# Residual products and the first tiles behind them by token halves, with half norms between

## The chip, the cores and the metric

The kernel runs on one core of a Trainium2 chip. The metric is the device time of one launch in microseconds (us). The core has five engines that run their own instruction queues: TensorE (PE, matrix products; its weight loads are listed as PEld), VectorE (DVE), ScalarE (ACT), GpSimd (POOL) and SyncE (SP, which here issues all DMAs).

## What is computed

One step of a diffusion backbone: two layers over 640 tokens (128 of context, 512 latent), width 1024. Each layer is

```
h = h + gate_a * Mixer(RMSNorm(h) * (1 + scale_a) + shift_a)
h = h + gate_f * SwiGLU(RMSNorm(h) * (1 + scale_f) + shift_f)
```

and a final RMSNorm gives the output. Scale, shift and gate have one value per channel for the context tokens and one for the latent ones. The mixer projects the normed input to many column tiles (`misc`, `mq`, `ckv`, ...), runs three branches (latent attention, gated linear attention, gated DeltaNet) and ends in an output projection (`wo`). The feed-forward part multiplies by 2 x 2816 columns (`fg`, `fu`) and back by `fo`. All of it is in float32.

## The kernel before

Activations lie transposed: channels on the 128 partitions, 640 tokens along the free dimension. The residual `h` is eight tiles of 128x640. A token half is 320 columns, `HS[0]` and `HS[1]`; half 0 holds the 128 context tokens and 192 latent ones, so an operation with a per-channel factor needs two pieces there (128 and 192 columns) and one (320) in half 1 (`PIECES`).

A float32 product is made of three float32r products: the weight tile is split into a rounded part `wh` (ACT, L465) and the residue `wl` (POOL, L466), the activations into `xh` and `xl`, and `mm_k` (L469) issues xh*wh, xl*wh, xh*wl for each token half and each 128 rows of depth.

`Stream` (L284) holds all large products as a list of units in a fixed order. A unit is up to four depth steps of one output tile, for one token half (c is 0 or 1) or for both (c is None), and it uses one block of weights of 128x512. `step` emits one depth step, `to(name)` emits until that tile is done and its post-operation is emitted, `steps(n)` emits n steps. Blocks are loaded by DMA into three buffers `wr` (on the SP queue) and split into three buffer pairs `wh`, `wl`; `ahead` (L319) splits one block ahead. Products write to a ring of three PSUM tiles of two banks. A unit with halves "in" or "post" runs half 0 and then half 1 with the same weight blocks.

The order in which each engine takes its instructions is fixed before the run by the framework's planner, from the order of emission and from its own idea of when each instruction is ready. While the chip runs, each engine's queue is strictly in order.

A residual product is followed by a norm that the next product needs. There are four such joins: `wo` to `fg0` in each layer, `fo1` of layer 0 to `misc` of layer 1, and `fo1` of layer 1 to the final norm and the output. Before the change a join goes like this (`resid_posts` L640, `join` L655):

- tiles 0 to 6 of the residual product run whole; after each, `h_update` (L637, DVE, reads PSUM) adds it to `h`, `Norm.add` squares it (L597, ACT) and adds the square to `nacc` (L598, DVE). `prescale` (L613, ACT) multiplies the tile by the next scale; at the `fo1` joins this is done in place, and in layer 0 only after `h` has been written to DRAM (`hsp`).
- tile 7 runs by halves. After each half: `h_update` of the half, its square (L602, ACT), two products with a matrix of ones that sum over channels (`cs`, L607, PE), then 1/sqrt by a logarithm and an exponential (L486, L488, ACT, each with a load of its function table).
- `modulate` (L615) makes the next input, for each of eight tiles and each half: the product with 1/rms (L619 on DVE, for tiles 1, 3, 5 on POOL; L622 on DVE for tile 7), the shift and rounding to `xh` (L624, ACT), the residue `xl` (L631, DVE). At the last join the product with 1/rms (L1810) is the output and goes out by DMA.
- the first tile behind the join (`fg0` or `misc`) runs by halves with shared weight blocks, all others whole.

In layer 0 `ModVe` (L549, DVE) also computes modulation values beside `wo0` to `wo4`, and `mod_fix` (L564, L567) finishes them before `prescale` can start.

Of the kernel before, what the change touches and what calls it, by code (L numbers as in the profile page):

```python
# [30 lines left out]
GROUPS = ((0, 11), (11, 22))  # L31

# [247 lines left out]
def mark(s):  # L280
    pass


class Stream:  # L284
    """Matrix products in a fixed order, emitted piece by piece between other work."""

    def __init__(self, pieces, load, split, psum, mm, ring):
# [3 lines left out]
        for name, ap, k0, kn, xs, c, first, last, post in pieces:  # L291
            if (name, k0) not in seen:
                seen[name, k0] = len(self.subs)
                self.subs.append((ap, kn))
                self.uses.append(0)
            i = seen[name, k0]
            self.uses[i] += 1
            self.units.append((name, i, k0, kn, xs, c, last, post))
# [20 lines left out]
    def ahead(self):  # L319
        i, c = self.units[self.u][1], self.units[self.u][5]  # L320
        self._split(i)
        top = max(self.w)
        for j in range(1, 3):
            self._load(top + j)
        if len(self.w) < self.ring and (top == i or c == 1):
            self._split(top + 1)

    def step(self):
# [8 lines left out]
        if self.k == kn:  # L337
# [5 lines left out]
            if last and (ph or c in (None, 1)):  # L343
                ps = self.ps[name] if c == 0 else self.ps.pop(name)
                ps = ps[:, :, :HF]
                with self.prio("pp"):
                    if ph:
                        self.posts[name](ps, c)
                    else:
                        self.posts.pop(name)(ps)  # L350
                if c != 0:
                    self.done.add(name)
                else:
                    self.done.add(name + "/0")
        return 0.82 if c is None else 0.41

    def steps(self, n):
        for _ in range(n):
            self.step()
# [13 lines left out]
def tile_hybrid(ctx: ExitStack, tc, a):  # L373
# [127 lines left out]
    # ---- modulation  # L501
# [20 lines left out]
    class ModVe:  # L522
        """Products of the condition with rows of the modulation weights, in single steps of the vector engine."""
# [59 lines left out]
    # ---- residual, norms  # L583
# [3 lines left out]
    class Norm:  # L587
        def __init__(self):
            self.acc = sp.tile([P, T], F32, name="nacc", tag="nacc", bufs=1)
            self.ps = self.last = None  # L590
# [8 lines left out]

        def end(self, h, c):  # L600
# [3 lines left out]
        def fin(self, c):  # L604
            self.ps = psg("cs") if self.ps is None else self.ps
            for i, t in enumerate((self.acc, self.last)):
                pe.matmul(self.ps[:, c, :HF], ones, t[:, HS[c]], start=(i == 0), stop=(i == 1))  # L607
            rstd_from(self.ps[:, c, :HF], self.acc[:, HS[c]], 1.0 / D, epsD[:, 0:1])

    def prescale(us, hs, sc, ds=range(7)):  # L610
        for d in ds:
            for i, s, e in ((0, 0, TP), (1, TP, T)):
# [27 lines left out]
    def resid_posts(names, hs, g, nm, keep=False):  # L640
        def post(ps, c=None, d=0):
            if d < 7:
                h_update(hs, d, ps, g)
                nm.add(d, hs[d])
                if keep:
                    dma(hsp[d], hs[d])
            else:
                h_update(hs, d, ps, g, (c,))
                nm.end(hs[d], c)
                if keep:  # L650
                    dma(hsp[d][:, HS[c]], hs[d][:, HS[c]])
        for d in range(8):
            G.posts[names[d]] = lambda ps, c=None, d=d: post(ps, c, d)

    def join(name, hs, nm, after, pre=None):  # L655
        """The last residual tile, the norm and its use, by halves of the tokens."""
        if pre:
            pre()
        G.to(name + "/0")
        G.steps(5)  # L660
        nm.fin(0)
        G.to(name)
        after(0, range(4))
        nm.fin(1)
        after(0, range(4, 8))
        after(1, range(8))

    # ---- DRAM scratch
# [8 lines left out]
    # ---- gated DeltaNet  # L677
# [142 lines left out]
    def turn_pairs(src, dst, scale):  # L820
        """Both heads of a pair from channels to tokens, chunk by chunk."""
# [13 lines left out]
    def gdn_solve(lp):  # L835
        Bb = lp.tile([P, 10, P], F32, name="Bb")
        ge.memset(Bb, 0.0)
        for d in range(2):
# [26 lines left out]
            for f in range(2):  # L865
# [11 lines left out]
                def narrow(w):  # L877
                    """Bb[:, g].T @ w[:, g] for all g, by the narrow operand and a turn."""
# [150 lines left out]
    # ---- latent attention  # L1029
# [225 lines left out]
    # ---- gated linear attention  # L1255
# [184 lines left out]
    # ---- the order of the large products  # L1440
    pieces = []

    def job(name, src, kt, xs, halves=None, ks=None):
        ks = ks or [(k0, min(4, kt - k0)) for k0 in range(0, kt, 4)]
        for c in ((0, 1) if halves else (None,)):
            for k0, kn in ks:
                pieces.append((name, src[:, k0 * P:(k0 + kn) * P], k0, kn, xs, c, k0 == 0, k0 + kn == kt, halves == "post"))

    for l in range(L):
        def k8(n, halves=None, ks=None, l=l):  # L1450
# [9 lines left out]
        else:  # L1460
            k8("misc", "in")
            k8("mq0")
# [24 lines left out]
        for d in range(8):  # L1487
            k8(f"wo{d}", "post" if d == 7 else None)
        for gi, (f0, f1) in enumerate(GROUPS):
            for f in range(f0, f1):  # L1490
                k8(f"fg{f}", "in" if f == 0 else None)
                k8(f"fu{f}")
            for d in range(8):
                job(f"fo{gi}_{d}.{l}", a["wfo"][l, d, :, f0 * P:f1 * P], f1 - f0, ("a",),
                    "post" if (gi, d) == (1, 7) else None)
# [42 lines left out]
    # ---- the layers  # L1538
# [36 lines left out]
    for l in range(L):  # L1575
# [166 lines left out]
        resid_posts([f"wo{d}.{l}" for d in range(8)], hs, mod[:, 16:24], nm)  # L1742
        for d in range(7):
            G.to(f"wo{d}.{l}")
            if l == 0:
                mv.run(0, range(16 + OPT["mc"] + (24 - OPT["mc"]) * min(d, 5) // 5, 16 + OPT["mc"] + (24 - OPT["mc"]) * min(d + 1, 5) // 5))
        if l == 0:
            mod_fix(mod, prm, 3)
            mod_fix(mod, prm, 4)
        mark(f"normf{l}")  # L1750
# [93 lines left out]
```

## Time and profile before

| what | value |
|---|---|
| median of 3 runs | 2895.22 us (2894.1 to 2898.76) |
| span of the profiled execution | 2896.0 us; no other time is listed for it |
| busy PE / PEld / DVE / ACT / POOL | 94% / 86% / 53% / 42% / 41% |
| mean granted TensorE clock | 0.968 |
| DMA | 317.10 MB, mean 109 GB/s |

Busy times are shares of the span. Products on PE overlap, so a busy PE is not a PE at its full rate: how many it does is read from when the tiles end. The granted clock is 1.00 at 2.4 GHz and 0.50 at 1.2 GHz.

### The profile page before, as it was taken

What the parts mean: (1) busy time and instruction counts of PE and PEld (TensorE: products, weight loads), DVE (VectorE), ACT (ScalarE), POOL (GpSimd) and SP (SyncE); (2) the same over time, 40 slices, a digit from 0 to 9 for tenths busy, and PEclk for the clock granted to TensorE, in tenths of its full rate; (3) what the DMA queues carried; (4) which work ended last, traced back from release to release, by engine and by line L of the source; (5) the groups of instructions that cost most, each with busy time, mean ns of one, the idle gap of its engine ahead of it and who ended that gap; (6) DMA issues with size and microseconds to landing.
All of it is one profiled execution on the core that took longest, in us unless ns stands there. A gap on an engine that the chain in (4) does not pass through costs nothing. (4 is left out here: it accounts for less than half of the span.)

```text
span 2896.0 us, 49763 instructions
## 1 busy us (share of the span) xinstructions
PE 2721.4 (94%) x19444; PEld 2498.5 (86%) x19444; DVE 1542.6 (53%) x2834; ACT 1209.0 (42%) x2276; POOL 1196.0 (41%) x872
## 2 busy tenths in 40 slices
PE   7899999889999999999998899987999999999998
PEld 4788888778779899999988888876877898999998
DVE  4765584747655699177358576556334334211212
ACT  5575655543333522122366645554333344222223
POOL 3543222333325467366445323233333264443443
PEclk9999999999999999999999999998999999999999
DMA  6254433245433355344323534332423231222222
GB/s 207 90 161 141 91 82 94 88 130 168 140 101 127 108 189 177 86 139 156 105 84 110 177 90 97 72 93 73 137 79 88 73 111 59 77 73 78 73 74 83
DMA packets 291834, 317.10 MB, mean 109 GB/s; under 512 B 163696, under 2 KB 174768, under 8 KB 291472
## 3 DMA queue, kind: packets, MB, share of 16 engines
q1 hardware_dynamic: 291600, 313.92, 37.3%
q8 instruction: 154, 2.52, 0.4%
q14 instruction: 80, 0.66, 0.1%
HBM read 266.01 MB, written 47.82 MB: 108 GB/s over the span
## 5 line engine op out<-in xcount | busy, mean ns | idle before, releaser
L466 POOL TENSOR_TENSOR wl<-wr,wh 128x512 fp32r<-128x512 f32 (+1 forms) x576 | 813.9, 1416 | 1307.0 <-ACT wh L465 1177.0
L474 PE MATMUL gm<-xh,wh 128*128 128x320 f32 x3456 | 846.2, 322 | 25.1 <-ACT xh L624 9.4
L474 PE MATMUL gm<-xh,wl 128*128 128x320 f32 x3456 | 826.8, 316 | 13.4 <-POOL wl L466 13.4
L474 PE MATMUL gm<-xl,wh 128*128 128x320 f32 x3456 | 832.5, 317 | 7.2 <-DVE xl L631 4.2
L465 ACT ACTIVATE wh<-wr 128x512 fp32r<-128x512 f32 (+1 forms) x576 | 357.6, 623 | 944.0 <-PE gm L474 648.9
L474 PEld LDWEIGHTS gm<-xh,wh 128*128 128x128 f32 x3456 | 589.6, 192 | 52.5 <-ACT xh L624 14.5
L474 PEld LDWEIGHTS gm<-xl,wh 128*128 128x128 f32 x3456 | 594.3, 192 | 25.0 <-DVE xl L631 9.8
L474 PEld LDWEIGHTS gm<-xh,wl 128*128 128x128 f32 x3456 | 592.6, 192 | 21.7 <-POOL wl L466 15.5
L549 DVE CUSTOM_DVE_ANT_0 ctb<-wmt,cbb 128x1024 f32<-128x1024 f32 (+1 forms) x200 | 298.6, 1493 | 3.4
L637 DVE SCALAR_TENSOR_TENSOR h<-gm,mod,h 128x128 f32<-128x128 f32 x144 | 55.7, 462 | 272.2 <-PE gm L474 266.1
L474 PE MATMUL gm<-ah,wh 128*128 128x320 f32 x704 | 164.6, 310 | 0.5 <-DVE h L637 0.5
L474 PE MATMUL gm<-ah,wl 128*128 128x320 f32 x704 | 164.1, 309 | 0.0
L474 PE MATMUL gm<-al,wh 128*128 128x320 f32 x704 | 163.9, 309 | 0.0
L962 ACT ACTIVATE VN<-ch 64x64 f32<-64x64 f32 x320 | 70.0, 219 | 178.5 <-DVE vs L959 164.5
L474 PEld LDWEIGHTS gm<-ah,wh 128*128 128x128 f32 x704 | 118.7, 188 | 1.6 <-DVE h L637 1.5
L474 PEld LDWEIGHTS gm<-al,wh 128*128 128x128 f32 x704 | 118.5, 188 | 0.2
L474 PEld LDWEIGHTS gm<-ah,wl 128*128 128x128 f32 x704 | 118.5, 188 | 0.0
L1773 DVE TENSOR_TENSOR th<-th,gm 128x640 f32<-128x640 f32 x44 | 36.2, 822 | 149.2 <-PE gm L474 148.4
L1766 DVE SCALAR_TENSOR_TENSOR th<-th,gm 128x640 f32<-128x640 f32 x44 | 35.9, 816 | 138.3 <-ACT th L1765 138.3
L479 POOL TENSOR_TENSOR al<-th,ah 128x640 fp32r<-128x640 f32 x44 | 89.5, 2033 | 28.0 <-DVE ah L478 28.0
L474 PE MATMUL gm<-ol,wh 128*128 128x320 f32 x384 | 99.3, 332 | 1.5 <-POOL ol L479 1.5
L474 PE MATMUL gm<-oh,wh 128*128 128x320 f32 x384 | 98.7, 334 | 0.5 <-DVE gth L1524 0.3
(747 smaller groups left out, 3822.8 us busy)
## 6 DMA issues: line engine op xcount, KB each, us to landing
wr<-in_wall_dram SPq DMA_DIRECT2D x432, 256.0 KB, 3.0
wmt<-in_wmodt_dram SPq DMA_DIRECT2D x60, 512.0 KB, 3.7
wr<-in_wfo_dram SPq DMA_DIRECT2D x64, 256.0 KB, 2.6
wr<-in_wbr_dram SPq DMA_DIRECT2D x48, 256.0 KB, 2.7
wmt<-in_wmodt_dram SPq DMA_DIRECT2D x40, 256.0 KB, 3.2
wm<-in_wmod_dram SPq DMA_DIRECT2D x16, 512.0 KB, 8.3
wr<-in_wfo_dram SPq DMA_DIRECT2D x32, 192.0 KB, 2.4
h<-in_xt_dram SPq DMA_DIRECT2D x16, 320.0 KB, 5.5
```

The lines of the kernel that those rows point to most:

```text
L465: se.activation(wh[:, :w], wr[:, :w], AF.Copy)
L466: ge.tensor_tensor(wl[:, :w], wr[:, :w], wh[:, :w], op=ALU.subtract)
L474: pe.matmul(ps[:, c, :HF], w_[:, wsl], x_[kx][:, c * HF:(c + 1) * HF], start=(start and i == 0), stop=(stop and i == 2))
L479: (lo or ge).tensor_tensor(dst_l, src, dst_h, op=ALU.subtract)
L549: ins = ve.tensor_tensor_reduce(self.t, wm, self.c[:, i], 0.5, 0.0, ALU.mult, ALU.add, accum_out=acc[h][:, m - m0, i:i + 1])
L637: ve.scalar_tensor_tensor(hs[d][:, s:e], ps[:, c, s - c * HF:e - c * HF], g[:, d, i:i + 1], hs[d][:, s:e], op0=ALU.mult, op1=ALU.add)
L962: se.activation(VN[d * 64:(d + 1) * 64, h, n], ps[h * 64:(h + 1) * 64, 1], AF.Copy)
L1766: ve.scalar_tensor_tensor(v3(th), v3(th), 1.0, ps, op0=ALU.add, op1=ALU.mult)
L1773: ve.tensor_tensor(v3(th), v3(th), ps, op=ALU.mult)
```

## The change

The last three tiles of each residual product (`NHV = 3`) run by halves: half 0 of tiles 5, 6, 7, then half 1 of tiles 5, 6, 7. Each half has its own PSUM tile, its own post-operation and its own copy of the weight blocks (the key of a block now holds the half). Likewise the first two tiles behind a join run as half 0 of both, then half 1 of both, again with their own copies of the blocks: `fg0` and `fu0`, and `misc` and `mq0` in layer 1. After each half of tiles 5 and 6 its square is added to `nacc` by half (`Norm.part`) and the half is prescaled. `join` now emits half 0's norm one depth step into half 1 of tile 5, all eight tiles of half 0's `modulate` between the next steps, and half 1's norm and `modulate` after half 1 of tile 7. `ahead` splits two blocks ahead for units by halves. The sums of the norm go to the small PSUM pool.

```diff
     def ahead(self):
...
-        if len(self.w) < self.ring and (top == i or c == 1):
-            self._split(top + 1)
+        want = i + (1 if c is None else 2)
+        while len(self.w) < self.ring and max(self.w) < want and max(self.w) + 1 < len(self.subs):
+            self._split(max(self.w) + 1)
...
+        def part(self, h, c):
+            sq = tmp()
+            se.activation(sq[:, HS[c]], h[:, HS[c]], AF.Square)
+            ve.tensor_tensor(self.acc[:, HS[c]], self.acc[:, HS[c]], sq[:, HS[c]], op=ALU.add)
...
-    def join(name, hs, nm, after, pre=None):
-        if pre:
-            pre()
-        G.to(name + "/0")
-        G.steps(5)
+    def join(name, l, nm, after):
+        G.to(f"{name}7.{l}:0")
+        G.steps(1)
         nm.fin(0)
-        G.to(name)
-        after(0, range(4))
+        for i in range(4):
+            after(0, range(2 * i, 2 * i + 2))
+            G.steps(2)
+        G.to(f"{name}7.{l}:1")
+        G.steps(1)
         nm.fin(1)
-        after(0, range(4, 8))
         after(1, range(8))
...
+    def by_halves(jobs, own):
+        for c in range(2):
+            for name, src, kt, xs in jobs:
+                for k0 in range(0, kt, 4):
+                    kn = min(4, kt - k0)
+                    key = f"{name}:{c}"
+                    pieces.append((key if own else name, src[:, k0 * P:(k0 + kn) * P], k0, kn, xs, c, k0 + kn == kt, own, key))
...
-        for d in range(8):
-            k8(f"wo{d}", "post" if d == 7 else None)
+        for d in range(8 - NHV):
+            k8(f"wo{d}")
+        by_halves([w8(f"wo{d}") for d in range(8 - NHV, 8)], True)
         for gi, (f0, f1) in enumerate(GROUPS):
...
+            if gi == 0:
+                by_halves([w8("fg0"), w8("fu0")], False)
```

## Rows read from the trace of the kernel before

**Rows 1.** The page: busy time of PE, and the granted clock in 40 slices.
```profile
PE 2721.4 (94%) x19444; PEld 2498.5 (86%) x19444; DVE 1542.6 (53%) x2834; ACT 1209.0 (42%) x2276; POOL 1196.0 (41%) x872
PEclk9999999999999999999999999998999999999999
```

**Rows 2.** Windows at layer 1's `wo` join: length, busy time by engine, clock, DMA.
```profile
2380.00:2403.00 23.00, 22.65 (x150) 21.72 (x148) 6.65 (x15) 11.32 (x19) 7.79 (x6) 1.00 0.23 66
2403.00:2432.00 29.00, 23.57 (x104) 19.45 (x105) 18.36 (x38) 18.43 (x37) 11.31 (x10) 0.76 0.15 43
```

**Rows 3.** Timeline of DVE there: start, duration, instruction, idle time before it.
```profile
2380.21 1.14 DVE L637 SCALAR_TENSOR_TENSOR h<-gm,mod,h 128x128 f32<-128x128 f32 x3 [4.28 <-PE gm L474]
2387.25 1.14 DVE L637 SCALAR_TENSOR_TENSOR h<-gm,mod,h 128x128 f32<-128x128 f32 x3 [4.28 <-PE gm L474]
...
2397.82 0.68 DVE L637 SCALAR_TENSOR_TENSOR h<-gm,mod,h 128x128 f32<-128x128 f32 x2 [0.76 <-PE gm L474]
...
2405.32 0.49 DVE L619 TENSOR_TENSOR th<-us,nacc 128x320 f32<-128x320 f32 x1 [1.85 <-ACT nacc L488]
...
2424.40 1.68 DVE L631 SCALAR_TENSOR_TENSOR xl<-th,mod,xh 128x320 fp32r<-128x320 f32 x2 [1.18 <-ACT xh L624]
...
2431.70 0.82 DVE L1773 TENSOR_TENSOR th<-th,gm 128x640 f32<-128x640 f32 x1 [2.91 <-PE gm L474]
```

**Rows 4.** Timeline of ACT there: the square of a half.
```profile
2398.53 0.47 ACT L602 ACTIVATE th<-h 128x320 f32<-128x320 f32 x1 [1.71 <-DVE h L637]
```

**Rows 5.** Windows of the modulate stage, layer 1's `wo` join and `misc` join.
```profile
2405.00:2426.10 21.10, 16.86 (x62) 13.26 (x63) 16.77 (x35) 14.11 (x31) 7.49 (x7) 0.68 0.04 12
1456.00:1477.30 21.30, 17.09 (x63) 13.84 (x63) 18.98 (x36) 15.08 (x33) 8.82 (x9) 0.68 0.12 36
```

**Rows 6.** The same windows, weight residues (L466) on POOL alone.
```profile
2405.00:2426.10 21.10, 1.28 (x1) 0.68 0.04 12
1456.00:1477.30 21.30, 3.08 (x3) 0.68 0.12 36
```

**Rows 7.** Tile `wr`, 2375 to 2405 us: splits (ns) and DMA landing.
```profile
L465 ACT ACTIVATE wh<-wr x8: 620/632/632, 2376.4 to 2402.9; 128x512 fp32r<-128x512 f32 x8
L466 POOL TENSOR_TENSOR wl<-wr,wh x8: 1261/1296/1306, 2377.2 to 2403.6; 128x512 fp32r<-128x512 f32 x8
DMA to landing us min/median/max: 2.5/2.6/3.0
```

**Rows 8.** Timeline of DVE at layer 0's `wo` join.
```profile
952.02 1.14 DVE L637 SCALAR_TENSOR_TENSOR h<-gm,mod,h 128x128 f32<-128x128 f32 x3 [0.66 <-PE gm L474]
...
1002.62 0.82 DVE L1773 TENSOR_TENSOR th<-th,gm 128x640 f32<-128x640 f32 x1 [2.91 <-PE gm L474]
```

**Rows 9.** Timeline of ACT at that join: the first prescale.
```profile
958.62 1.31 ACT L613 ACTIVATE us<-h,mod 128x128 f32<-128x128 f32 x3 [2.69 <-DVE mod L567]
```

**Rows 10.** Timeline of DVE at the `misc` join (layer 0's `fo1`).
```profile
1425.03 1.14 DVE L637 SCALAR_TENSOR_TENSOR h<-gm,mod,h 128x128 f32<-128x128 f32 x3 [6.91 <-PE gm L474]
...
1449.23 0.68 DVE L637 SCALAR_TENSOR_TENSOR h<-gm,mod,h 128x128 f32<-128x128 f32 x2 [2.08 <-PE gm L474]
1456.78 1.20 DVE L619 TENSOR_TENSOR th<-h,nacc 128x320 f32<-128x320 f32 x1 [0.59 <-ACT nacc L488]
1475.54 1.70 DVE L631 SCALAR_TENSOR_TENSOR xl<-th,mod,xh 128x320 fp32r<-128x320 f32 x2 [1.15 <-ACT xh L624]
```

**Rows 11.** Timeline of ACT there: prescale, then the copies of `misc` and `mq0`.
```profile
1450.06 1.02 ACT L613 ACTIVATE h<-h,mod 128x128 f32<-128x128 f32 x2 [3.76 <-DMA hsp<-h]
1478.40 0.69 ACT L1598 ACTIVATE misc<-gm 128x640 f32<-128x640 f32 x1
1485.52 0.69 ACT L1618 ACTIVATE th<-gm 128x640 f32<-128x640 f32 x1
```

**Rows 12.** Timeline of PE and DVE near the end.
```profile
2878.16 0.41 PE L474 MATMUL gm<-ah,wh 128*128 128x320 f32 x1 [0.23 <-DVE h L637]
2883.96 0.55 DVE L637 SCALAR_TENSOR_TENSOR h<-gm,mod,h 128x320 f32<-128x320 f32 x1
```

More of the change, by code (lines that the diff above doesn't have):

```diff
@@ L31 @@
 GROUPS = ((0, 11), (11, 22))
+NHV = 3
 O_MQ, O_CKV, O_KR = 0, 256, 384
@@ L290, in __init__ @@
         seen = {}
-        for name, ap, k0, kn, xs, c, first, last, post in pieces:
-            if (name, k0) not in seen:
-                seen[name, k0] = len(self.subs)
+        for name, ap, k0, kn, xs, c, last, post, key in pieces:
+            if (key, k0) not in seen:
+                seen[key, k0] = len(self.subs)
                 self.subs.append((ap, kn))
                 self.uses.append(0)
-            i = seen[name, k0]
+            i = seen[key, k0]
             self.uses[i] += 1
@@ L358, in steps @@
         for _ in range(n):
-            self.step()
+            if self.u < len(self.units):
+                self.step()
     def fill(self, us):
@@ L1460, in tile_hybrid @@
         else:
-            k8("misc", "in")
-            k8("mq0")
+            by_halves([w8("misc"), w8("mq0")], False)
             k8("mq1")
@@ L1741, in tile_hybrid @@
         nm = Norm()
[L1742 to L1750, printed above, removed]
         with pool("us", "left") as up:
             us = [up.tile([P, T], F32, name=f"us{d}") for d in range(7)]
-            join(f"wo7.{l}", hs, nm, lambda c, ds: modulate(hs, nm.acc, mod[:, 32:40], mod[:, 24:32], c, ds, us),
-                 lambda: prescale(us, hs, mod[:, 32:40]))
+            resid_posts("wo", l, hs, mod[:, 16:24], nm,
+                        halved=lambda d, c: prescale(us, hs, mod[:, 32:40], range(d, min(d + 1, 7)), c))
+            for d in range(8 - NHV):
+                G.to(f"wo{d}.{l}")
+                if l == 0:
+                    mv.run(0, range(16 + OPT["mc"] + (24 - OPT["mc"]) * min(d, 5) // 5, 16 + OPT["mc"] + (24 - OPT["mc"]) * min(d + 1, 5) // 5))
+            if l == 0:
+                mod_fix(mod, prm, 3)
+                mod_fix(mod, prm, 4)
+            mark(f"normf{l}")
+            prescale(us, hs, mod[:, 32:40], range(8 - NHV))
+            join("wo", l, nm, lambda c, ds: modulate(hs, nm.acc, mod[:, 32:40], mod[:, 24:32], c, ds, us))
         with pool("fp", "left") as fp:
@@ L1797, in tile_hybrid @@
                 m2 = mods[l + 1]
-                join(f"fo1_7.{l}", hs, nm, lambda c, ds: modulate(hs, nm.acc, m2[:, 8:16], m2[:, 0:8], c, ds, hs[:7]),
-                     lambda: prescale(hs, hs, m2[:, 8:16]))
+                G.to(f"fo1_{7 - NHV}.{l}")
+                prescale(hs, hs, sc_n, range(8 - NHV))
+                join("fo1_", l, nm, lambda c, ds: modulate(hs, nm.acc, m2[:, 8:16], m2[:, 0:8], c, ds, hs[:7]))
             else:
@@ L1811, in result @@
                         dma(a["yt"][d][:, HS[c]], t[:, HS[c]])
-                def scaled():
-                    for d in range(7):
-                        se.activation(hs[d], hs[d], AF.Copy, scale=fn[:, d:d + 1])
-                join(f"fo1_7.{l}", hs, nm, result, scaled)
+                G.to(f"fo1_{7 - NHV}.{l}")
+                prescale(hs, hs, sc_n, range(8 - NHV))
+                join("fo1_", l, nm, result)
         mvctx.__exit__(None, None, None)
```

80 lines of the change are left out of this document (44 added, 36 removed).

## The prediction

> **What bounds the kernel now.** I read the page first. PE is busy for 94% of the span, and its clock stands at 9 in nearly every slice [rows 1]; the other engines are near half or below. So time can only be won where PE does not run at its full rate, and the four joins are such places. The windows show it next: in the 23 us ahead of layer 1's `wo` join PE handles 150 products at a clock of 1.00, in the 29 us behind it 104 at 0.76, while DVE rises from 6.65 to 18.36 us and ACT from 11.32 to 18.43 [rows 2]. Then the timeline of DVE gives the steps of a join, because `h_update` starts as soon as a tile is done. Two whole `wo` tiles end 7.04 us apart [rows 3]: 48 products, 0.1467 us each. This is the full rate.
>
> From the end of `wo4` (2380.21) to the end of `fu0` (2431.70) pass 51.5 us [rows 3]. The 240 products in it need 240 x 0.1467 = 35.2 us; 16.3 us are lost. The same rows divide the time:
>
> - A, tiles 5, 6 and half 0 of tile 7: 2380.21 to 2397.82, 17.6 us, PE at full rate.
> - B, half 0's chain (update, square, sums, logarithm, exponential): to 2405.32, 7.5 us. PE does half 1 of tile 7 under it.
> - C, `modulate` of both halves: to 2424.40 + 1.68 = 2426.08, 20.8 us. DVE is busy for 16.8 of 21.1 us, ACT for 14.1, PE's clock is 0.68 [rows 5]. DVE and its exchange with ACT set the pace; PE waits for each `xh` and `xl`.
> - D, what PE still has to do: to 2431.70, 5.6 us.
>
> Layer 0's `wo` join takes 50.6 us between the same points [rows 8]. The `misc` join, from the end of `fo1_4` (1425.03), takes 53.4 us to the end of `misc` and 60.5 us to that of `mq0` [rows 10, 11].
>
> **The change part by part.** I go by layer 1's `wo` join and then say what differs at the others.
>
> A shrinks: half 0's chain starts after 72 products, 72 x 0.1467 = 10.6 us instead of 17.6. That is the gain, 7.0 us; the products taken out are not saved, they now lie under B and C, where PE had idle time.
>
> B keeps its instructions. Under it ACT gets a half square of tile 5 (0.47, as in [rows 4]), a half prescale of about the same size, and weight splits: a block now serves 12 products, 1.76 us, instead of 3.52, so some 2 splits more of 0.63 [rows 7]. That is 2.2 us more on ACT, in order, in a chain that also waits for DVE and PE. Between 0 and 2.2 I take 1.0, since the chain leaves gaps: B = 8.5. The sums of half 0 are now emitted one depth step into half 1 of tile 5. Behind a late square, PE has the rest of half 1 queued; but PE then has 10.6 us of products for 8.5 us of chain plus the first of C, so this wait costs nothing unless it passes 2 us.
>
> C keeps all of `modulate` and gains two things on DVE. First, the updates of half 1 of tiles 6 and 7 (0.55 each [rows 12]) and one half addition (0.49, as a 128x320 product in [rows 3]): 1.6 us. Second, the weights. The join has 10 blocks more than before: 6 for `wo5` to `wo7`, 4 for `fg0` and `fu0`. When C begins, 8.5 us after half 0 of tile 7, PE has used 8.5 / 1.76 = 4.8 blocks of half 1 and two are split ahead, so 7 of the 14 blocks that follow half 0 are still to be split, against one in the window of before [rows 6]. What a residue on POOL does to DVE the trace shows by comparison: the stage at the `misc` join has 3 residues instead of 1 and the same `modulate`, and DVE is busy for 18.98 us instead of 16.77 [rows 5, 6]. That is 1.1 us of DVE for each residue; the stage was no longer for it (20.8 us there too, less 0.3), because DVE had idle time. With 6 more residues, 6.6 us, that idle time is used up: 16.8 + 1.6 + 6.6 = 25.0 us with DVE never idle. Below this stands 20.8 (all of it falls into idle time), above it 20.8 + 1.6 + 6.6 = 29.0 (the idle time stays). I take 25.0, the nearest to what the two stages show. Half 1's chain starts when PE ends half 1 of tile 7, 10.6 + 1 us after half 0, and needs 8.5: it is done about 20 us after half 0. C's half 0, with two pieces a tile, is more than half of 25.0 and lasts until 8.5 + 12.5 = 21 at least. So it is hidden, but only if its sums are not queued on PE behind a depth step of `fg0` that waits for a late `xl`.
>
> D shrinks. The last `xl` releases one depth step of `fg0` and then half 1 of `fu0`: 27 x 0.1467 = 4.0 us, instead of 5.6.
>
> The supply of weights: a `wr` buffer comes round after DMA 2.6, ACT 0.63 and POOL 1.30 us, with 0.2 for hand-over 4.7 us [rows 7]; three buffers give a block each 1.6 us, PE wants one each 1.76. It holds as long as the queues of ACT and POOL add less than 0.5 us to a round. Four blocks of start (two split, two loaded) cover 7 us; I cost it at nothing, and at 1 to 2 us a join if the table loads on ACT stand in its way.
>
> Sum for this join: 10.6 + 8.5 + 25.0 + 4.0 = 48.1 against 51.5, 3.4 us less.
>
> Layer 0's `wo` join: the factors of `prescale` exist only at 958.62 [rows 9]. Five tiles at an estimated 1.0 us (three short pieces took 1.31 there; a tile has a short and a long one) and three splits bring ACT to 965.5; half 0 of tile 7 is now done at 952.02 + 10.6 = 962.6 and updated at 963.4. The planner may put the square first, but prescale stands ahead of it in the emission, so B is 2 us longer: 50.1 against 50.6, 0.5 us less.
>
> `misc` join: tiles have 11 depth steps, so A falls from 24.2 us (1425.03 to 1449.23) to 99 x 0.1467 = 14.5. B is 8.5 and 1.0 more: the prescale in place waits for the write of `h` to DRAM, and ACT stood 3.76 us behind such a write [rows 11]; there are now four such waits by halves, in the same queue as the splits. C is 25.0, D 4.0. `mq0` ends after 53.0 instead of 60.5 us, 7.5 less; but `misc`, which the gates behind it read, now ends only 3.5 us ahead of it (24 products) where it was 7.1: 49.5 against 53.4, 3.9 less. PE and the chain of gates share the next stage; I take the middle, 5.7. The writes of `h` are now half size and twice as many on SP between the weight loads; covered by the blocks ahead.
>
> Final join: no product follows. Half 1's chain stays as it is. PE no longer waits for the update of half 0 in its own PSUM tile (0.23 [rows 12]), and half 0's output products no longer stand in front of half 1's update: 0.3 us less.
>
> All: 0.5 + 5.7 + 3.4 + 0.3 = 9.9 us less. The span of 2896.0 becomes 2886.1; it lies 0.8 above the median of 2895.22, so the median becomes 2885.
>
> **The rivals.** *The residues are hidden.* C is 22.4 (20.8 + 1.6), as the `misc` stage suggests, where two more cost no length: 2.6 us less at three joins, 2877. Against it: DVE has only 4.3 us of idle time in that window, and 6.6 are to go in.
>
> *The idle time stays.* DVE's gaps are waits for ACT, and ACT has more to do as well: C is 29.0, 4.0 us more at three joins: 2897, no change.
>
> *POOL and DVE shut each other out, slower than before.* The place is C: each of the 7 residues holds DVE for its whole 1.30 us [rows 7] on top of a stage whose gaps stay, 20.8 + 1.6 + 9.1 = 31.5, 6.5 us more at three joins, 19.5 in all: 2905. It decides from about 1.0 us of stage length for each residue (three joins give 9.6 us, 3.2 each, to lose: C = 28.2, less 22.4, by 6). For it: 1.1 us of DVE for a residue of 1.30 [rows 5 to 7]. Against it: DVE busy grew by 2.2 us at the `misc` join and the stage did not. The Trainium skill (SBUF — State Buffer, "SBUF: two separate sides") says that a DVE operation with two SBUF inputs and a GpSimd operation take a shared pair of ports as an exclusive lock, held for a whole instruction, and that the other one fully blocks. By that rule each residue that meets a product of `modulate` costs all of its rest, and the sum would be the 2905 of this rival; the 1.1 of 1.30 us agrees with the lock, the unchanged stage length does not with its full price.
>
> *It does not overlap.* The planner's fixed order puts half 0's chain behind half 1's work on ACT or DVE; then A does not shrink and only the weights are added: about 2897.
>
> **How the numbers follow.** Forecast (C near 25) 0.42, hidden 0.22, idle stays 0.20, shut out 0.12, no overlap 0.04. For the forecast alone 2879 to 2889. The range takes in the hidden case with room for B at its low end, 2870, and the idle that stays, up to 2900; some 0.18 is left out. A difference of 0.2%, 5.8 us, is what can be told from no change. Faster: the hidden case and nearly all of the forecast, 0.61. Within 0.2%: the rest of the forecast and most of the two cases at 2897, 0.23. Slower: 0.16.
>
> **What would show it.** Right: from the end of `wo4` to that of `fu0` some 48 us in layer 1; the first L619 some 19 us after the end of `wo4`; DVE above 23 us busy in C; 42 more splits on L465 and L466. Wrong: PE waiting on `wl` (L466) or `wh` inside half 1 of tiles 5 to 7; half 1's sums late behind `fg0`; a C shorter than 22 or longer than 28 us; a gain or loss away from the joins, where nothing was costed, from the planner's new order.

## The result and the profile after

The changed kernel takes 2923.72 us (median of 4 runs, 2918.0 to 2929.86) against 2894.68 before: a ratio of 1.0096 (95% interval 1.0081 to 1.0112; intervals stand in square brackets below), 29 us slower. The forecast was 2885 with a range of 2870 to 2900: the change went the other way, and past the range. The profiled execution took 2918.0 us, the fastest of the four; its span is 2916.2, 20.2 more than before. So the two traces can speak of 20 of the 29 us.

First the page of the changed kernel (busy time by engine, then the clock in 40 slices). Against [rows 1] PE is busy for the same time and the clock stands as high, so nothing is lost in PE's own work. DVE has 23.5 us more, ACT and POOL have more too.

```profile
PE 2723.3 (93%) x19444; PEld 2503.7 (86%) x19444; DVE 1566.1 (54%) x2842; ACT 1237.2 (42%) x2341; POOL 1251.2 (43%) x914
PEclk9999999989999899999999999999999999999999
```

The marks of the prediction, read from the timelines of DVE and ACT, give this table (us; before / forecast / measured): A up to half 0 of tile 7, B half 0's chain, C `modulate`, D what PE still has to do. At `misc` D runs to the end of the `misc` tile, for which the prediction gave no D; the time to the end of `mq0` stands in the last column.

| join | A | B | C | D | whole | to `mq0` |
|---|---|---|---|---|---|---|
| `wo`, layer 0 | 17.6 / 10.6 / 10.6 | 7.5 / 10.5 / 14.4 | 19.9 / 25.0 / 32.1 | 5.6 / 4.0 / 3.2 | 50.6 / 50.1 / 60.3 | |
| `misc` | 24.2 / 14.5 / 14.6 | 7.5 / 9.5 / 7.2 | 20.5 / 25.0 / 35.7 | 1.2 / – / 1.1 | 53.4 / 49.5 / 58.5 | 60.5 / 53.0 / 63.6 |
| `wo`, layer 1 | 17.6 / 10.6 / 10.6 | 7.5 / 8.5 / 5.4 | 20.8 / 25.0 / 33.3 | 5.6 / 4.0 / 3.3 | 51.5 / 48.1 / 52.5 | |
| last (from `fo1_4`'s update to the last output) | | | | | 39.3 / 39.0 / 45.3 | |

The joins lose 9.7 + 3.1 (at `mq0`) + 1.0 + 6.0 = 19.8 us, nearly all of the 20.2 by which the span grew. A is what was forecast, to 0.1 us. C is 7 to 11 us longer than forecast, at all three joins.

Windows of layer 1's `wo` join in the changed kernel (columns as in [rows 2]): A, B, C; under them the weight residues (L460) on POOL in C alone, and the shifted residue products (L630) on DVE. C takes 33.4 us instead of 21.1 [rows 5]; DVE is busy for 26.90 instead of 16.77, and idle for 6.5. There are 10 weight residues in it instead of 1 [rows 6], and the 24 pieces of L630 take 18.35 us (11.32 for the same 24 before, L631 there). The forecast had DVE busy for 25.0 us and never idle: 1.9 of the 8.4 us in excess are work, 6.5 are idle time, of which 4.6 stand in one place.

```profile
2393.00:2404.00 11.00, 11.00 (x78) 11.00 (x77) 5.49 (x11) 7.64 (x16) 7.87 (x6) 1.00 0.42 129
2403.90:2409.30 5.40, 5.40 (x35) 4.98 (x34) 1.27 (x4) 5.17 (x8) 2.71 (x3) 1.00 0.45 128
2409.20:2442.60 33.40, 25.34 (x128) 21.81 (x126) 26.90 (x39) 21.17 (x44) 19.48 (x16) 0.85 0.26 82
2409.20:2442.60 33.40, 13.36 (x10) 0.85 0.26 82
2409.20:2442.60 33.40, 18.35 (x24) 0.85 0.26 82
```

DVE's timeline there answers to [rows 3]. Half 0 ends at 2403.90, 10.56 us after tile 4, and its first L618 starts at 2409.26. But half 1's first L618 (2431.39) waits 4.59 us for `nacc`, its own 1/rms: the chain that the prediction had hidden ends last. At the other two inner joins this wait is 5.6 us (layer 0) and 5.9 (`misc`).

```profile
2393.34 1.14 DVE L636 SCALAR_TENSOR_TENSOR h<-gm,mod,h 128x128 f32<-128x128 f32 x3 [4.27 <-PE gm L468]
2403.90 0.67 DVE L636 SCALAR_TENSOR_TENSOR h<-gm,mod,h 128x128 f32<-128x128 f32 x2 [1.27 <-PE gm L468]
2408.62 0.55 DVE L636 SCALAR_TENSOR_TENSOR h<-gm,mod,h 128x320 f32<-128x320 f32 x1 [4.04 <-PE gm L468]
2409.26 0.49 DVE L618 TENSOR_TENSOR th<-us,nacc 128x320 f32<-128x320 f32 x1
2410.53 3.05 DVE L630 SCALAR_TENSOR_TENSOR xl<-th,mod,xh 128x128 fp32r<-128x128 f32 x3 [0.77 <-ACT xh L623]
...
2422.32 0.54 DVE L636 SCALAR_TENSOR_TENSOR h<-gm,mod,h 128x320 f32<-128x320 f32 x1
...
2425.70 1.11 DVE L597 TENSOR_TENSOR nacc<-nacc,th 128x320 f32<-128x320 f32 x2
2431.39 1.55 DVE L618 TENSOR_TENSOR th<-us,nacc 128x320 f32<-128x320 f32 x2 [4.59 <-ACT nacc L482]
2433.23 1.19 DVE L630 SCALAR_TENSOR_TENSOR xl<-th,mod,xh 128x320 fp32r<-128x320 f32 x1 [0.28 <-ACT xh L623]
```

PE and ACT show why. PE starts the last of half 1's 72 products at 2416.69; tile 7's update, ready then, has its place in DVE's queue at 2422.32, between pieces of half 0's `modulate`. And half 1 of tile 5 was added to `h` at 2408.62, but its square (the first L596) runs on ACT at 2424.43, behind half 0's work there. Then the tables, logarithm and exponential follow, and `nacc` is there at 2431.4.

```profile
2416.69 0.41 PE L468 MATMUL gm<-xh,wl 128*128 128x320 f32 x1 [0.78 <-POOL wl L460]
...
2423.79 0.74 ACT L623 ACTIVATE xh<-th,mod 128x128 fp32r<-128x128 f32 x2
2424.43 0.45 ACT L596 ACTIVATE th<-h 128x320 f32<-128x320 f32 x1
2425.81 0.47 ACT L596 ACTIVATE th<-h 128x320 f32<-128x320 f32 x1 [0.93 <-DVE xl L630]
...
2427.20 1.28 ACT L480 ACT_TABLE_LOAD   x1
2429.05 0.53 ACT L480 ACTIVATE nacc<-cs,epsD 128x320 f32<-128x320 f32 x1 [0.56 <-PE cs L606]
2429.59 1.28 ACT L482 ACT_TABLE_LOAD   x1
2430.89 0.47 ACT L482 ACTIVATE nacc<-nacc 128x320 f32<-128x320 f32 x1
```

POOL beside DVE's 3.05 us: the three pieces of L630 that began at 2410.53 (0.34 us for 128 columns and 0.41 for 192 where nothing is beside them) end at 2413.58, 0.16 us behind the second of these two residues. The two residues cost them some 2 us.

```profile
2410.44 1.29 POOL L460 TENSOR_TENSOR wl<-wr,wh 128x512 fp32r<-128x512 f32 x1
2412.13 1.29 POOL L460 TENSOR_TENSOR wl<-wr,wh 128x512 fp32r<-128x512 f32 x1 [0.40 <-POOL wl L460]
```

Layer 0's `wo` join on ACT, beside [rows 9]: ten prescale pieces in a row, 4.63 us, before the weight split at 965.73. PE waits 3.4 us for that `wh`, and half 0's logarithm is only at 974.01 (a wait of 1.49 for the sums on PE): B is 14.4 us.

```profile
961.19 4.63 ACT L612 ACTIVATE us<-h,mod 128x128 f32<-128x128 f32 x10 [0.59 <-DVE mod L561]
965.73 0.61 ACT L459 ACTIVATE wh<-wr 128x512 fp32r<-128x512 f32 x1
...
974.01 0.53 ACT L480 ACTIVATE nacc<-cs,epsD 128x320 f32<-128x320 f32 x1 [1.49 <-PE cs L606]
```

The last join on DVE, beside [rows 12], and SP under it. All outputs of half 0 (L1842, L1839) stand ahead of the update of half 1 of tile 5 at 2893.45, and their eight writes, 6.71 us on SP's queue, ahead of the last two weight loads. Tile 7 is updated at 2903.54 after DVE stood idle for 7.04 us.

```profile
2886.66 5.36 DVE L1842 TENSOR_TENSOR h<-h,nacc 128x320 f32<-128x320 f32 x5 [4.68 <-ACT nacc L482]
2891.94 1.58 DVE L1839 SCALAR_TENSOR_TENSOR h<-h,fn,nacc 128x320 f32<-128x320 f32 x1
2893.45 0.54 DVE L636 SCALAR_TENSOR_TENSOR h<-gm,mod,h 128x320 f32<-128x320 f32 x1
...
2903.54 0.55 DVE L636 SCALAR_TENSOR_TENSOR h<-gm,mod,h 128x320 f32<-128x320 f32 x1 [7.04 <-PE gm L468]
```

```profile
2887.18 6.71 SPq L383 DMA_DIRECT2D out_yt_dram<-h  x8
2893.98 0.88 SPq L383 DMA_DIRECT2D wr<-in_wfo_dram  x2
```

### The profile page after: what moved, and what is told of

Its sections match the earlier page's. It is cut to its first block, busy times and chain, and to the rows that moved or that the text cites. A ratio compares the mean times of both kernels' runs of the same rounds, so it can differ in the third digit from the quotient of the medians.

```text
span 2916.2 us, 50068 instructions
## 1 busy us (share of the span) xinstructions
PE 2723.3 (93%) x19444; PEld 2503.7 (86%) x19444; DVE 1566.1 (54%) x2842; ACT 1237.2 (42%) x2341; POOL 1251.2 (43%) x914
## 5 line engine op out<-in xcount | busy, mean ns | idle before, releaser
L460 POOL TENSOR_TENSOR wl<-wr,wh 128x512 fp32r<-128x512 f32 (+1 forms) x618 | 868.7, 1409 | 1290.0 <-ACT wh L459 1143.4
L468 PE MATMUL gm<-xh,wh 128*128 128x320 f32 x3456 | 855.1, 322 | 30.7 <-ACT xh L623 9.8
L468 PE MATMUL gm<-xl,wh 128*128 128x320 f32 x3456 | 842.2, 318 | 16.2 <-DVE xl L630 13.1
L468 PE MATMUL gm<-xh,wl 128*128 128x320 f32 x3456 | 838.4, 317 | 12.2 <-POOL wl L460 12.2
L459 ACT ACTIVATE wh<-wr 128x512 fp32r<-128x512 f32 (+1 forms) x618 | 382.3, 622 | 919.5 <-PE gm L468 619.3
L636 DVE SCALAR_TENSOR_TENSOR h<-gm,mod,h 128x128 f32<-128x128 f32 (+2 forms) x144 | 56.4, 460 | 247.9 <-PE gm L468 242.0
L468 PE MATMUL gm<-ah,wl 128*128 128x320 f32 x704 | 172.4, 311 | 3.7 <-POOL wl L460 3.7
L468 PE MATMUL gm<-ah,wh 128*128 128x320 f32 x704 | 172.8, 311 | 0.2 <-ACT wh L459 0.2
L468 PE MATMUL gm<-al,wh 128*128 128x320 f32 x704 | 171.7, 310 | 0.0
```

The source lines that it names most:

```text
L459: se.activation(wh[:, :w], wr[:, :w], AF.Copy)
L460: ge.tensor_tensor(wl[:, :w], wr[:, :w], wh[:, :w], op=ALU.subtract)
L468: pe.matmul(ps[:, c, :HF], w_[:, wsl], x_[kx][:, c * HF:(c + 1) * HF], start=(start and i == 0), stop=(stop and i == 2))
L636: ve.scalar_tensor_tensor(hs[d][:, s:e], ps[:, c, s - c * HF:e - c * HF], g[:, d, i:i + 1], hs[d][:, s:e], op0=ALU.mult, op1=ALU.add)
```

## The experiments

In the expectations T1 is the theory that half 1 comes late through its place in the order, T2 that the weight copies cost, T3 that ACT's prescale block at layer 0's `wo` does. Ratios are to the kernel before on the same chip; differences to the changed kernel are to its median of 2923.7, whose four runs spread over 12 us, so that some 5 us of difference can't be told from none by the time alone. The traces are steadier at the joins (A of layer 1's `wo` join is 10.56 us in every kernel here with three tiles by halves) than between them: the stretch up to `wo4` of layer 0, which these edits leave alone, takes from 948.3 to 955.9 us. So the marks of each join are given beside the time.

**Own buffers for the half squares.** `part` took its scratch tile from the ring of three `th` buffers that `modulate` uses.

```diff
-            sq = tmp()
-            se.activation(sq[:, HS[c]], h[:, HS[c]], AF.Square)
+            sq = self.pool.tile([P, HF], F32, name="sqh", tag="sqh", bufs=2)
+            se.activation(sq, h[:, HS[c]], AF.Square)
...
```

> The changed kernel with one edit: the half squares of tiles 5 and 6 (L596) get two buffers of their own instead of the three 'th' buffers that modulate uses too. Theory 1 (half 1's norm is late because these squares stand behind all of half 0's modulate, for a 'th' buffer and by their place in the emission; DVE then stood idle for 5.6, 5.9 and 4.6 us at the three inner joins): the squares move ahead, the update and square of tile 7's half 1 do not, so about half of the idle time goes, 2 to 3 us a join, 2915 to 2919 by median, nothing at the final join. Theory 2 (the copies of the weights stretch modulate, POOL's residues hold DVE): no change, 2922 to 2926.

2919.65 us, 1.008 [1.0063, 1.0097]: 4 us less, between the two expectations and not told from no change by the time alone. DVE's wait ahead of half 1 fell from 5.6 to 3.7 us in layer 0, from 4.6 to 2.4 in layer 1, from 5.9 to 4.4 at `misc`. In layer 1 the squares of tiles 5 and 6 now run among half 0's work, at 2411.58 and 2417.35; what is left is tile 7's update, at 2424.34 on DVE. The buffer is a part of the delay, and not the main one.

**Half 1 emitted first.** The join emits the rest of the residual product ahead of half 0's `modulate`, instead of two depth steps between its parts.

```diff
-        for i in range(4):
-            after(0, range(2 * i, 2 * i + 2))
-            G.steps(2)
         G.to(f"{name}7.{l}:1")
+        after(0, range(8))
         G.steps(1)
         nm.fin(1)
```

> The changed kernel with one edit in join: all steps of half 1 of tiles 5 to 7, and so their updates, squares and sums, are emitted ahead of half 0's modulate (and ahead of half 0's output at the final join) instead of behind it. Theory 1: the idle time of DVE ahead of half 1's modulate goes, 4 to 6 us at each of three joins, and at the final join the weight loads no longer stand behind half 0's output on SP, 6 us: 2900 to 2906 by median. Theory 2: the stage is as long as before, at most the 6 us of the final join: 2917 to 2920.

2910.07, 1.0048 [1.0033, 1.0063]: 13.7 us less. T1's sign is right; its size was put at least 4 us too high. In layer 1 (window of C, then DVE) the wait ahead of half 1 is 1.43 us and C is 28.2 (28.6 in layer 0, 29.1 at `misc`); DVE is busy in the window for 24.34 us and idle for 4.0, as it was before (4.3, [rows 5]).

```profile
2414.80:2443.10 28.30, 21.11 (x108) 17.10 (x106) 24.34 (x38) 18.75 (x39) 18.19 (x15) 0.94 0.28 86
```

```profile
2430.01 0.49 DVE L618 TENSOR_TENSOR th<-us,nacc 128x320 f32<-128x320 f32 x1 [1.43 <-ACT nacc L482]
```

But a wait now stands ahead of half 0. Its 1/rms is there at 2411.52, when the exponential ends, and DVE takes the first product at 2414.90: ahead of it in DVE's queue stands the update of half 1 of tile 6, which waits for PE. This is 1.7 us in layer 0, 6.3 at `misc` and 3.4 in layer 1, where B grows from 5.4 to 8.7. So the three inner joins win only 2.3, 0.7 (to `mq0`) and 2.3 us.

```profile
2411.05 0.47 ACT L482 ACTIVATE nacc<-nacc 128x320 f32<-128x320 f32 x1
```

```profile
2414.43 0.55 DVE L636 SCALAR_TENSOR_TENSOR h<-gm,mod,h 128x320 f32<-128x320 f32 x1 [0.67 <-PE gm L468]
2414.90 0.48 DVE L618 TENSOR_TENSOR th<-us,nacc 128x320 f32<-128x320 f32 x1
```

The last join falls from 45.3 to 40.3 us: of the eight writes now one stands ahead of the last two weight loads.

```profile
2887.38 0.34 SPq L383 DMA_DIRECT2D out_yt_dram<-h  x1
2890.68 1.56 SPq L383 DMA_DIRECT2D wr<-in_wfo_dram  x2
2892.29 3.74 SPq L383 DMA_DIRECT2D out_yt_dram<-h  x7
```

**No residue for half 1's copies.**

```diff
-                self.subs.append((ap, kn))
+                self.subs.append((ap, kn, c != 1))
...
+            if not lo:
+                return wh, wh
             wl = wp.tile([P, 512], F32R, name="wl", tag="wl")
...
```

> The changed kernel without the residue (POOL) of the weight copies that only half 1 uses; the product with it takes the rounded weights instead, so the count of products and of ACT's splits stays and the count of residues on POOL is that of the kernel before (576). This leaves out part of the computation. Theory 2: 9 or 10 residues fewer at each join, 5 to 7 of them inside the modulate stage at 1.1 us of DVE each: 5 to 7 us a join less, 15 to 20 in all, 2904 to 2909 by median. Theory 1: the idle time ahead of half 1's modulate stays (4.6 to 5.9 us), at most 1 us a join: 2920 to 2924.

2900.45, 1.0015 [1.0006, 1.0025]: 23.3 us less for 42 residues (638 on POOL become the 596 of the kernel before), 0.55 each, more than T2 gave. The wait ahead of half 1 stays (4.95 in layer 0, 4.26 at `misc`, 5.06 in layer 1), so this part is a cost of its own. By the marks the joins are 4.6, 6.6 (to `mq0`), 4.7 and, at the last, 4.5 us shorter. The last has no `modulate`: there half 0's output products on DVE, 6.9 us in the changed kernel, take 4.0.

**The stage behind the join whole** (`misc`, `fg0`, `fu0` as before; 12 copies fewer).

```diff
-            by_halves([w8("misc"), w8("mq0")], False)
+            k8("misc", "in")
+            k8("mq0")
...
-            if gi == 0:
-                by_halves([w8("fg0"), w8("fu0")], False)
-            for f in range(max(f0, 1), f1):
-                k8(f"fg{f}")
+            for f in range(f0, f1):
+                k8(f"fg{f}", "in" if f == 0 else None)
```

> The changed kernel with the first two tiles behind each join as they were before the change (misc and fg0 by halves with shared weights, mq0 and fu0 whole); the residual tiles stay by halves. Theory 1: the idle time ahead of half 1's modulate stays, and PE loses what it could do for half 0 of the second tile, about 2 us a join: 2925 to 2932 by median. Theory 2: 4 blocks fewer at three joins, 4 us of DVE each, against the same 2 us: 2914 to 2920.

2915.71, 1.0066 [1.0051, 1.0081]: 8.0 us less, as T2 has it. By the marks C falls by 3.4, 3.2 and 2.8 us, but D grows by 3 us at the `wo` joins, and all joins together are only 1.9 us shorter; where the rest lies is not shown.

**Both: half 1 first, and no residues for its copies** (the two edits above together).

> Both edits together: half 1's steps emitted ahead of half 0's modulate, and no residue for the copies that only half 1 uses (the product with it takes the rounded weights, which leaves out part of the computation). Alone they took 13.7 and 23.3 us off the changed kernel's median of 2923.7. If the late half 1 (theory 1) and POOL's residues (theory 2) are two separate costs, they add up: 2883 to 2891, faster than the kernel before by about what was forecast. If they are one cost seen twice (the residues are what makes half 1 late), little is added to the larger: 2896 to 2901.

2895.47, 1.0003 [0.9991, 1.0014]: 28.3 us less, where the two alone give 13.7 + 23.3 = 37; the time lies between the two expectations, next to that of one cost. They overlap by a quarter. By the marks (10.3 and 20.4 us alone, 23.5 together) 3.1 us of the overlap lie at the last join, where both shorten the same wait. C is now 24.2, 25.4 and 24.4 us, near the 25.0 of the forecast. Against the kernel with half 1 first alone, layer 1's window has 4 residues instead of 9; DVE is busy for 3.6 us less and the stage is 3.8 us shorter. At this load a residue costs 0.7 us of DVE, and all of it is length (0.9 us of C for each in layer 0, 0.6 at `misc`). Layer 1's join takes 46.8 us, 1.3 less than forecast; B is still 16.4 us in layer 0 and 14.3 at `misc`, and these two joins take 54.2 and 58.4 (to `mq0`) instead of 50.1 and 53.0.

```profile
2399.10:2423.60 24.50, 19.64 (x107) 16.68 (x106) 20.77 (x38) 18.42 (x39) 11.76 (x10) 0.93 0.30 93
```

**Layer 0's prescale of tiles 0 to 4 emitted behind half 0's sums.**

```diff
         nm.fin(0)
+        if pre:
+            pre()
...
-            prescale(us, hs, mod[:, 32:40], range(8 - NHV))
+            scaled = lambda: prescale(us, hs, mod[:, 32:40], range(8 - NHV))
+            if l:
+                scaled()
...
```

> The changed kernel with one edit at layer 0's wo join: the prescale of tiles 0 to 4 is emitted behind half 0's sums instead of ahead of half 0's tiles 5 to 7. In the changed kernel ten of its pieces held ACT for 4.6 us at 961 us, weight splits and squares behind them, and PE waited 3.4 us for a split. Theory 3 (this block is what makes layer 0's wo join lose 9.8 us where layer 1's loses 1.0): 4 to 7 us less, 2917 to 2920 by median. Theories 1 and 2 alone (that join is like layer 1's): no change, 2922 to 2926.

2919.73, 1.0075 [1.0056, 1.0094]: 4.0 us less, as T3 has it, though by the time alone not told from no change. The join falls from 60.3 to 55.2 us and B from 14.4 to 7.9. On ACT the splits now stand between the prescale pieces, and half 0's square at 966.88 ahead of the table load.

```profile
964.02 0.61 ACT L459 ACTIVATE wh<-wr 128x512 fp32r<-128x512 f32 x1
964.54 1.62 ACT L612 ACTIVATE us<-h,mod 128x512 f32<-128x512 f32 x3
...
966.58 0.39 ACT L612 ACTIVATE us<-h,mod 128x128 f32<-128x128 f32 x1
966.88 0.46 ACT L601 ACTIVATE th<-h 128x320 f32<-128x320 f32 x1
```

**The kernel before, with a copy of the weights for each half** where it already ran by halves (16 copies, no other change).

```diff
+            key = (name, k0, c if name != "misc.0" else None)
-            if (name, k0) not in seen:
-                seen[name, k0] = len(self.subs)
+            if key not in seen:
+                seen[key] = len(self.subs)
...
-            i = seen[name, k0]
+            i = seen[key]
```

> The kernel before, order and halves as they were, but each half of the tiles that it runs by halves (tile 7 of the residual products, fg0, and misc of layer 1) loads and splits its own copy of the weights: 16 blocks more, 2 of them in each modulate stage. Theory 2: 2 to 3 us a join at the three inner joins, 2901 to 2905 by median. Theory 1 (only the order is at fault, copies are hidden): 2894 to 2897.

2900.32, 1.0011 [1.0001, 1.0021]: 3.5 us more, just under what T2 gave; 0.22 for each copy, but only two of the 16 fall into each of the three C. C grows by 2.3 us in layer 0 and by 1.4 at `misc` and in layer 1, 0.7 to 1.1 for each residue. In layer 1's window three residues stand instead of one [rows 6]; DVE has 2.4 us more and the stage is 1.2 longer than in [rows 5]. So about half of the first residues' cost is hidden in DVE's idle time there; in layer 0 next to none is.

```profile
2405.50:2427.80 22.30, 16.84 (x59) 12.09 (x60) 19.18 (x35) 15.19 (x33) 11.03 (x9) 0.69 0.12 35
```

**Half 1 first and the next stage whole** (the two edits above together).

> Half 1 emitted first, and the first two tiles behind a join as before the change; only the residual tiles 5 to 7 by halves with their own copies. Alone the two edits took 13.7 and 8.0 us off 2923.7. If they add up: 2900 to 2904. If the whole second tile costs PE its work under half 1's modulate once that is no longer late: 2906 to 2911.

2901.82, 1.0017 [1.0005, 1.0029]: 21.9 less; 13.7 + 8.0 = 21.7, these two add up.

**The same, with the prescales late**: layer 0's as above, and those of half 1 of tiles 5 and 6 behind half 0's `modulate`.

```diff
-                        halved=lambda d, c: prescale(us, hs, mod[:, 32:40], range(d, min(d + 1, 7)), c))
+                        halved=lambda d, c: c or prescale(us, hs, mod[:, 32:40], range(d, min(d + 1, 7)), c))
...
         after(0, range(8))
         G.steps(1)
         nm.fin(1)
+        late()
...
```

> Half 1 first, the tiles behind the joins whole (as e8_first_and_whole, 2901.8 us), and in addition no prescale ahead of a half's norm: at layer 0's wo join tiles 0 to 4 are prescaled behind half 0's sums, and at all joins half 1 of tiles 5 and 6 is prescaled behind half 0's modulate. In e8 half 0's chain still took 15.3 us at layer 0's wo join and 15.8 at the misc join, where layer 1's wo join takes 8.7. Theory 3 (prescales, which at the misc join wait for the write of h to DRAM, stand ahead of the chain in ACT's queue): both chains fall to 8 or 9 us; some of it is lost again because half 1's part of the stage does not start earlier, 3 to 6 us gained at each: 2890 to 2896 by median. Otherwise: 2899 to 2904.

2901.33, 1.0022 [1.001, 1.0035]: no gain. The `wo` join of layer 0 is 2.8 us shorter than without the edit. The prescales of half 0 of tiles 5 and 6 stay where they were, though, so that at `misc` ACT still waits 2.78 us for the write of `h`, with half 0's square behind it, and that join is 2.9 us longer.

**Two tiles by halves** (otherwise the last kernel; 20 copies more than the kernel before, where that one has 30).

```diff
-NHV = 3
+NHV = 2
```

> e9 with two residual tiles by halves (6 and 7) instead of three: two weight blocks fewer at a wo join, three at fo1, and half 0's chain starts 3.5 us (4.8 at fo1) later. Theory 2 (copies are what costs): 2 to 3 us a join back against 3.5 to 4.8 of head start, of which about half is used: within 3 us of e9. If the head start is worth its full price: 10 to 14 us above e9.

2890.38, 0.999 [0.9981, 1.0]: 11 us less than with three, a miss. The copies are not the reason: C falls from 24.8 to 21.6 us in layer 0, but only from 27.1 to 26.8 at `misc`, and it is 24.0 and 24.1 in layer 1. B falls by 3.7 us in layer 0, 9.9 at `misc` and 3.3 in layer 1, where A grows by 2.6, 4.8 and 3.5. With three tiles half 0's first product waits in DVE's queue behind half 1's update of tile 6, as in the kernel with half 1 first, for 3.5, 7.6 and 3.4 us; with two tiles for 0.0, 1.2 and 0.0. So the third tile's head start is used up in DVE's queue. By the marks the joins are 8.9 us shorter together.

**The next stage by halves again** (three tiles, prescales late; in the kernel with the prescales late, the edit of the whole next stage undone).

> e9 with the first two tiles behind each inner join by halves again, with their own copies (e2_half1_first plus the later prescales). Theory 2: four copies more at three joins, 2 to 4 us each, as between e8 and e2 (8.3 us): 6 to 10 us above e9. If the price was the late chain and not the copies: within 3 us of e9.

2911.25, 1.006 [1.0044, 1.0077]: 9.9 us more, for 12 copies and their order. C is 3.7, 4.6 and 4.2 us longer, but D 2 to 3 us shorter, and by the marks the joins are only 1.8 us longer together; as with the next stage whole in the changed kernel, the rest is not located.

**One tile by halves** (next stage whole, prescales late; 10 copies).

```diff
-NHV = 2
+NHV = 1
```

> e9 with one residual tile by halves (tile 7), as before the change, but with its own copies of two blocks (three at fo1) and its own PSUM tiles: 1 to 3 us above the kernel before by theory 2, at most the 0.23 us waits below it by theory 1.

2889.88, 0.9983 [0.9971, 0.9995]: 4.8 us below the kernel before, where 1 to 3 more was expected; with two tiles (2890.38) it is the lowest here, and the two can't be told apart. It takes no further tile out of A; at the `wo` joins it wins in B and C. In layer 1 half 0 ends at 2395.16 and the first L618 starts at 2400.52: 5.4 us instead of 7.5 [rows 3]. The sums stand one depth step into half 1, not five: in the kernel before the sum over half 0's last square starts at 2400.86, 1.9 us after that square ends [rows 4], here at 2396.40, 0.06 after it. No run moved the sums alone. C has 2 residues and is 19.5 us. The `wo` joins are 2.8 and 3.7 us shorter, those at `misc` and the end 2.8 and 1.2 longer, 2.4 us less together; the rest of the 4.8 lies between the joins, where the traces differ by more than that from run to run. That half 1's sums have a PSUM tile of their own here may help C; it was not tried alone.

```profile
2400.86 0.70 PE L607 MATMUL cs<-th,ones 128*128 128x320 f32 x2
```

```profile
2396.40 0.81 PE L606 MATMUL cs<-th,ones 128*128 128x320 f32 x2
```

```profile
2395.16 0.67 DVE L636 SCALAR_TENSOR_TENSOR h<-gm,mod,h 128x128 f32<-128x128 f32 x2 [0.76 <-PE gm L468]
2399.88 0.55 DVE L636 SCALAR_TENSOR_TENSOR h<-gm,mod,h 128x320 f32<-128x320 f32 x1 [4.04 <-PE gm L468]
2400.52 0.49 DVE L618 TENSOR_TENSOR th<-us,nacc 128x320 f32<-128x320 f32 x1
```

```profile
2400.40:2420.00 19.60, 15.24 (x63) 11.47 (x64) 17.80 (x36) 14.43 (x32) 8.94 (x8) 0.83 0.09 28
```

## Why the prediction was wrong

Against its 2886.1 us of span the changed kernel took 2916.2, 30.1 more. By the table that is 10.2 at layer 0's `wo`, 9.0 to 10.6 at `misc`, 4.4 at layer 1's `wo` and 6.3 at the end.

**Right: A, and D at the `wo` joins.** Tiles 5 to 7 give half 0 after 10.6 and 14.6 us as worked out, and D came out 0.7 to 0.8 us shorter than forecast. At `misc` the end of `mq0` came 6.1 us after C, not 4.0. The gain of 7.0 and 9.6 us in A is real; it is given back in C.

**Too high: B without the prescales.** The forecast had 8.5 and 9.5 us; 5.4 and 7.2 were measured. With the sums one step into half 1 layer 1's chain takes 5.4 us, in the last experiment as well, and the prediction did not count this, though it named the edit. The 1.0 us that it added for ACT's work under B is not seen in layer 1: half 1 of tile 5 is updated at 2408.62 only, when the chain is nearly done. That B is 8.7 us there with half 1 first, close to the 8.5, is luck: its last 3.4 us are DVE's queue.

**Failed: "So it is hidden" (half 1's chain).** The prediction gave half 1's chain the time from PE's end of the product to the end of half 0's `modulate`, and named only PE's queue as a danger. PE came close: it starts half 1's last product at 2416.69, 12.8 us after half 0's update, where 11.6 were counted. The prediction left out the other two queues. Of tile 5's half 1 one depth step is emitted ahead of half 0's `modulate` and two behind each quarter of it, so its eighth and last stands behind the whole; all updates and squares of half 1 are emitted there. The planner moved tile 5's update ahead, but left tile 7's on DVE at 2422.32 and the squares on ACT at 2424.43. The price is DVE idle for 5.6, 5.9 and 4.6 us. Emitting half 1 first takes it to 1.4 and wins 13.7 us in all, some 5 of which belong to the last join. It is no cure: 1.7, 6.3 and 3.4 us then stand ahead of half 0, behind half 1's updates in DVE's queue. No order that was tried with three tiles hides both.

**Failed: "that idle time is used up".** Six residues more, seven instead of one, were costed at 1.1 us of DVE each, and the 4.3 us of idle time were to vanish. With half 1's chain mostly out of the way (half 1 first) C is 28.2 us, DVE busy for 24.3 and idle for 4.0, 1.4 of them the wait that is left: DVE's work was sized well, the idle time stayed, and the rival "the idle time stays", with its 29.0, describes it. What is idle on DVE is its exchange with ACT; of two residues' 2.4 us it takes in 1.2 in layer 1 of the kernel before with copies, and from the fourth to the ninth nothing. The count was low, 10 and not 7 (9 in layer 0, 12 at `misc`), since a longer stage takes in more of them.

The choice rested on the `misc` stage, and that was misread. Of its three residues in [rows 6] one ends at 1456.26, ahead of the stage's first product at 1456.78 [rows 10]. And of the 2.2 us that DVE has more there, L631 has only 0.75 (12.07 us against 11.32); 0.7 are the first L619 alone, which takes 1.20 us [rows 10] instead of 0.49 [rows 3] and begins together with POOL's own product. So a residue cost DVE less there than was read off, and the 1.1 us, near the 0.8 to 1.2 that the experiments give, owe that to luck.

```profile
1454.99 1.27 POOL L466 TENSOR_TENSOR wl<-wr,wh 128x512 fp32r<-128x512 f32 x1 [1.07 <-ACT wh L465]
1456.77 0.86 POOL L619 TENSOR_TENSOR th<-h,nacc 128x320 f32<-128x320 f32 x1 [0.51 <-ACT nacc L488]
```

```profile
1456.00:1477.30 21.30, 12.07 (x24) 0.68 0.12 36
2405.00:2426.10 21.10, 11.32 (x24) 0.68 0.04 12
```

The rival "POOL and DVE shut each other out" put a residue's whole 1.30 us on the stage. The Trainium skill (SBUF — State Buffer, "SBUF: two separate sides") says that one of the two holds the shared ports for a whole instruction, and that the other is blocked meanwhile; the rows above where L630 ends 0.16 us behind the residue agree. The whole price was not paid: a residue cost 0.6 to 1.1 us of stage length. The 31.5 us of that rival were passed at all three joins, but with 4.6 to 5.9 us of the late chain in them; with half 1 first C is 28.2 to 29.1 us.

The supply of weights, costed at nothing, took little: inside half 1 of tiles 5 to 7 PE waited 0.8 us for a `wl` at each `wo` join and 1.7 at `misc`. The one long wait, for a `wh`, belongs to the next point.

**Mis-sized: the prescale at layer 0.** The prediction saw that ten pieces stand ahead in the emission and gave B 2 us for it. It counted the time of three splits on ACT and half 0's square behind them, not that PE waits for a split: PE stood 3.4 us for a `wh` that was queued behind the ten pieces, and the sums slipped behind that. The pieces also began at 961.19, not at 958.62. B was 14.4 instead of 10.5, and 7.9 once the pieces were moved.

**Failed: "Final join: ... 0.3 us less".** It was 6.0 more. Half 1 of three tiles now stands behind half 0's output on DVE, and its weight loads behind eight output writes on SP. The residues of half 1's copies stretch that output from 4.0 to 6.9 us; without them this join takes 40.8, with half 1 first 40.3, with both 38.8. The same step in which the prediction counted the writes of `h` at `misc` should have counted these.

**Not settled.** At `misc` no kernel that computes everything beats the kernel before; the waits for the writes of `h` on ACT are seen, and were not taken out alone. The 4 us of the own buffers and of the later prescale are within what runs of one kernel differ by; only the traces show an effect. Why the next stage whole is worth 8 to 10 us by the time and some 2 us by the marks is open.

## What to carry to other kernels

Work that is moved "under" another stage is hidden only if every engine takes it there: write down for each queue (ACT, DVE, SP, not PE alone) what is emitted ahead of it, and what it will stand ahead of: half 1 was late behind half 0, and half 0 was late behind half 1. A half that shares no weights costs the weights twice, in the stage where the exchange between two engines sets the pace; idle time inside such an exchange took in at most half of a third engine's work here. Before splitting more tiles, emit the dependent step earlier: with one depth step instead of five, B was 2 us shorter at the `wo` joins with no further tile split.

## What was not expected of the hardware

The price of a weight residue on POOL depends on where it is paid. Over the whole run it came to 0.22 us for each of 16 copies and 0.55 for each of 42. Where residues fall into `modulate`, C shows 0.7 to 1.1 us for each of the first (one to three, or two to four, in a stage) and 0.6 to 0.9 from four to nine or ten.

DVE's time is steadier than one line of it suggests. In layer 1's window the 24 pieces of the residue product took 11.32 us beside one residue, 13.25 beside four, 14.28 beside nine (half 1 first) and 18.35 beside ten (the changed kernel). But other operations of DVE are held too. All of its busy time, less the added updates and additions (about 2.0 us in the changed kernel, 1.2 with half 1 first), grew for each residue more by 1.2 us (copies in the kernel before), 1.0 (one tile by halves), 0.9 (half 1 first without residues for half 1), 0.8 (half 1 first) and 0.9 (the changed kernel).
